# Placing weight rounding, head scalings and gate loads in the mixer stage of a one-layer hybrid decoder trunk

## The chip, the cores and the metric

The kernel runs on one core of one Trainium2 chip. The metric is the device time of one execution in microseconds, as the median of several runs. A core has five engines with instruction queues of their own: TensorE (PE, matmuls; its weight loads are listed as PEld), VectorE (DVE), ScalarE (ACT), GpSimd (POOL) and SyncE (SP, which here issues most DMAs). They meet only at semaphores. Matmul results land in PSUM, which has eight banks here.

## The reference, cut to what matters

One decoder layer over 1024 tokens and 16 meta tokens, width 1024, in float32. The change touches the mixer, whose parts are four recurrent heads, four pooling groups, and two gated branch products that are added and projected:

```python
u = rmsnorm(h, mix_norm_pre[l])
proj = u @ w_in[l]
q, f_logit, i_in, g_out, v_pool, gate_a, gate_b = jnp.split(proj, cuts, axis=-1)
a = hgrn2(q, f_logit, i_in, g_out, lbs[l], hgrn_out_norm[l])   # 4 heads of 128, chunks of 64; rmsnorm per head, times sigmoid(g)
p = multiscale_pool(v_pool, pool_proj[l], pool_scale[l])       # 4 groups of 128
z = (jax.nn.sigmoid(gate_a.astype(jnp.float32)) * (a @ w_branch_hgrn[l])
     + jax.nn.sigmoid(gate_b.astype(jnp.float32)) * (p @ w_branch_pool[l]))
h = h + rmsnorm(z @ w_out[l], mix_norm_post[l])
u = rmsnorm(h, ffn_norm_pre[l])
gt = causal_dwconv(u @ ffn_w_gate[l], ffn_conv_w[l], ffn_conv_b[l])
y = (jax.nn.gelu(gt, approximate=True) * (u @ ffn_w_up[l])) @ ffn_w_down[l]
h = h + rmsnorm(y, ffn_norm_post[l])
```

## The kernel before

**Precision.** Each matmul operand is split into a rounded high part and a low part (fp32r): `hi` is a cast on ACT, `lo = x - hi` a subtraction on DVE. A product is then three matmuls (hi by hi, lo by hi, hi by lo). In the profile these are `whi`/`wlo` for weights, `ah`/`al` for the heads' outputs, `uhi` for the pooled projections (high and low part lie in one buffer), `rh`/`rl` for a head's squares, `zc` for the merged branches. This splitting of weights is called rounding here. `whi`, `wlo` and the unrounded `wraw` each have three buffers in rotation.

**The stage.** Between 325 and 562 us of the profiled execution a string, `ORDER`, sets in which sequence the kernel's code is written, and for PE also the sequence in which it runs: there PE runs under a manual schedule, while ACT, DVE and SP get their order from a scheduler that follows the written order and its own estimates. The words of the string:

- `h0` to `h3`: one step of a head's generator (`head_steps`, L656 to L812). Its levels multiply `q`, `k` by decays `f` on DVE (L681, L687, L689), PE makes `sl`, and DVE copies it into `near` (L719); later PE transposes k (`pt`, copied by ACT to `kt`, L760), builds `ds`, DVE adds it up in the states `st` (L779), and PE makes the output `po` (L796, L797), which ACT copies to `o` (L799). At the end ACT and DVE square and split, PE sums the squares (`ms`, L806), ACT takes Ln and Exp into `rs` (L808, L809), and DVE scales (`o *= rs`, L810).
- `PV`, `G`, `PP`: value and gate products and the pool projections. `PP`'s results have posts on ACT (L847) and DVE (L848).
- `BB`, `BA`: the 8 branch products of the pool side and the 8 of the head side, in column blocks of 128; a and b are their halves. Their weights come in pairs, one load for two products, rounded by `wsplit2` (L166 ACT, L167 DVE), three loads ahead. After each product DVE multiplies the gates by it (`post_branch`, L886). The gates (`sa`) are loaded from DRAM (`sscr`) by `load_gate`. BA's posts are followed by the sum of both branches (L1249, L1268).
- `sa0` to `sa3`: the split of a finished head's output into `ah` and `al` (L840, L841).
- `w0` to `w5`: steps that round weights of the later FFN and put them into DRAM (`kept0h` to `kept9l`), with ACT casts (L929), DVE subtractions and combinations (L927, L930) and stores on SP (L944).

After the last branch product, BA7, comes the mix: products `pm` of the merged branches with w_out, from 561 us.

Of the kernel before, what the change touches and what calls it, by code (L numbers as in the profile page):

```python
# [12 lines left out]
ALU = mybir.AluOpType  # L13
# [41 lines left out]

ORDER = ("h0 h1 PVp0 PVq0 h0 PVr0 h1 PVs0 h0 PVp1 h1 PVq1 h0 PVr1 h1 PVs1 h0 sp0 PVp2 h1 PVq2 h0 sp1 PVr2 h1 PVs2 "
# [4 lines left out]
POOLED = ()  # L61
VLOAD = 8
TRUNC = False
# [2 lines left out]
CH_Q = [(0, CW), (CW, CW), (2 * CW, CW)]  # L66


@with_exitstack
def trunk_kernel(ctx: ExitStack, tc: tile.TileContext, x, meta_tokens, mix_norm_pre,  # L70
                 mix_norm_post, w_in, hgrn_lower_bounds, hgrn_out_norm, w_branch_hgrn,
                 pool_proj, pool_scale, w_branch_pool, w_out, ffn_norm_pre, ffn_norm_post,
                 ffn_w_gate, ffn_w_up, ffn_conv_w, ffn_conv_b, ffn_w_down, out):
    nc = tc.nc
    act, dve, pool_e, pe = nc.scalar, nc.vector, nc.gpsimd, nc.tensor

    cnt = [0]
    const = ctx.enter_context(tc.tile_pool(name="const", bufs=1))
# [27 lines left out]
    def bank(name="ps"):  # L106
        return stage["ps", "p"].tile([P, 512], F32, tag="ps", name=nm(name))
# [14 lines left out]
    def rr(a):  # L122
        return a.bitcast(F32)
# [23 lines left out]
        return t  # L147


    def wsplit(src, n_k, n_c, eng=dve):  # L150
        raw = wst.tile([P, n_k * n_c], F32, tag="wraw", name=nm("wraw"), bufs=NRAW, padded_shape=[P, 1024])
        with tc.issue_after(stage["after"].ins) if "after" in stage else nullcontext():
            stage["load"] = nc.sync.dma_start(raw.rearrange("p (k c) -> p k c", k=n_k), src)
        hi = wst.tile([P, n_k * n_c], F32R, tag="whi", name=nm("whi"), padded_shape=[P, 1024])
        lo = wst.tile([P, n_k * n_c], F32R, tag="wlo", name=nm("wlo"), padded_shape=[P, 1024])
        act.copy(hi, raw)
        eng.tensor_tensor(lo, raw, rr(hi), ALU.subtract)
        return [(hi.rearrange("p (k c) -> p k c", k=n_k), lo.rearrange("p (k c) -> p k c", k=n_k))]

    def wsplit2(*srcs):  # L160

        raw, (hi, lo) = wraw_tile(), (wst.tile([P, 1024], F32R, tag=t, name=nm(t)) for t in ("whi", "wlo"))
        views = [[t[:, i * 512 : (i + 1) * 512].rearrange("p (k c) -> p k c", k=4) for t in (raw, hi, lo)] for i in range(2)]
        for (r, _, _), src in zip(views, srcs):
            stage["load"] = nc.sync.dma_start(r, src)
        act.copy(hi, raw)  # L166
        dve.tensor_tensor(lo, raw, rr(hi), ALU.subtract)  # L167
        return [(h, l) for _, h, l in views]

    class Loader:  # L170


        def __init__(self, srcs, get=wsplit, first=None):
            self.srcs, self.get, self.got, self.at = srcs, get, [], 0
            self.ahead(first)
# [5 lines left out]
        def next(self):  # L181
            self.at += 1
            return self.got[self.at - 1]
# [475 lines left out]
    def head_steps(h):  # L659
        f, k, kb, q = slot(NM + L, name="f"), slot(NM + L, name="k"), slot(NM + L, name="kb"), slot(NM + L, name="q")  # L660
# [122 lines left out]
        o, rs = slot(TQ, name="o"), slot(TQ, name="rs")  # L783
# [7 lines left out]
        for j in range(2):  # L791
            ps = bank("po")
            for i in range(4):
                c = 4 * j + i
                t = M0 + c * P
# [11 lines left out]
            pe.matmul(ps[:, :n], onesr, rl[:, lo : lo + n], start=False, stop=True)  # L807
            act.activation(rs[:, lo : lo + n], ps[:, :n], AF.Ln, bias=eps_t)  # L808
        act.activation(rs, rs, AF.Exp, scale=-0.5)  # L809
        dve.tensor_tensor(o, o, rs, ALU.mult)  # L810
        heads[h] = dict(o=o)


# [24 lines left out]
    def split(src, name, eng=dve):  # L838
        hi, lo_ = slot(TQ, F32R, name + "h"), slot(TQ, F32R, name + "l")
        act.copy(hi, src)  # L840
        eng.tensor_tensor(lo_, src, rr(hi), ALU.subtract)  # L841
        return hi, lo_
# [10 lines left out]
    sas, sbs, z = {}, {}, {}  # L853
# [64 lines left out]
    def keep(*what, lo=None):  # L918

        tiles_ = [wst.tile([P, 1024], F32R, tag="whi", name=nm("whi"))]  # L920
        tiles_.append(wst.tile([P, 1024], F32R, tag="wlo", name=nm("wlo")) if lo is None else lo)
        at = [KEPT.index(key) for key, _ in what]
        for i, (_, src) in enumerate(what):
            hi, lo = (t[:, i * 512 : (i + 1) * 512].rearrange("p (k c) -> p k c", k=4) for t in tiles_)
            if isinstance(src, tuple):
                for a, op, b in src:
                    dve.tensor_tensor(rr(lo), rr(lo) if a is None else a, rr(lo) if b is None else b, op)  # L927
                src = rr(lo)
            act.copy(hi, src)  # L929
            dve.tensor_tensor(lo, src, rr(hi), ALU.subtract)  # L930
        for h, t in enumerate(tiles_):
            if len(at) == 2 and at[1] == at[0] + 1 and at[0] % 2 == 0:
                owed.append((kept[at[0] // 2][h], rr(t)))
                continue
            for i, n in enumerate(at):
                c = (n % 2) * 512
                owed.append((kept[n // 2][h][:, c : c + 512], rr(t)[:, i * 512 : (i + 1) * 512]))
# [34 lines left out]
    order = ORDER.split()  # L972
    order = [(o_[:-1], int(o_[-1])) for o_ in order]
# [59 lines left out]
    with tc.manual_schedule(engines={E.Activation, E.DVE, E.PE}):  # L1033
# [131 lines left out]
        for h in range(EARLY_G):  # L1165
            src, n_k, xs, chunks, post = job("G", h)
# [37 lines left out]
    def split_z(c, k):  # L1204
        n = len(TILES[c]) * P
        a = HALO + TILES[c][0] * P
        zc = slot(2 * n + (2 * HALO if c == 0 else 0), F32R, "zc")
        zh, zl = zc[:, :n], zc[:, n : 2 * n]
        act.copy(zh, z[k][:, a : a + n])
        dve.tensor_tensor(zl, z[k][:, a : a + n], rr(zh), ALU.subtract)  # L1210
        if c == 0:
            zm = zc[:, 2 * n :]
            act.copy(zm[:, :HALO], z[k][:, :HALO])
            dve.tensor_tensor(zm[:, HALO:], z[k][:, :HALO], rr(zm[:, :HALO]), ALU.subtract)
            return zh, zl, zm
        return zh, zl
# [3 lines left out]
    with tc.manual_schedule(engines={E.PE}):  # L1220
        for kind, i in order:
            if kind == "sp":
                pool_split(i)
                continue
            if kind == "w":
                keep_first(i) if i < EARLY else next(keeps[i - EARLY])
                continue
            if kind == "sa":
                ahl[i] = split(heads[i]["o"], "a")
                continue  # L1230
            if kind == "h":
                if i not in gens:
                    gens[i] = head_steps(i)
                next(gens[i], None)
                if not loader.at and "after" in stage:
                    loader.ahead()
                continue
            kind, part = kind.rstrip("abpqrs"), kind[-1]
            src, n_k, xs, chunks, post = job(kind, i)
            if part in "qr":  # L1240
                next(halves_of[kind, i])
                continue
            if part in "bs":
                banks = next(halves_of[kind, i])
                loader.ahead()
                pay()
                after[kind, i] = post(banks)
                if kind == "BA":
                    dve.tensor_tensor(sas[i], sas[i], sbs[i], ALU.add)  # L1249
                    z[i] = sas[i]  # L1250
                continue
            if kind in ("BA", "BB"):
                load_gate(sas if kind == "BA" else sbs, kind == "BB", i)
            ws = loader.next()
            if (kind, i) == ("BA", KD - 1):
                z0 = [split_z(0, k) for k in range(ZA)]
            if part in "ap":
                halves_of[kind, i] = proj_parts(None, 0, n_k, xs, chunks, ws=ws, name="p" + kind.lower(),
                                                cuts=(n_k // 2,) if part == "a" else range(n_k // 4, n_k, n_k // 4))
                next(halves_of[kind, i])  # L1260
                continue
            banks = proj(None, 0, n_k, xs, chunks, ws=ws, name="p" + kind.lower(),
                         by_bank=2 if (kind, i) == ("BA", KD - 1) else 0)
            loader.ahead()
            pay()
            after[kind, i] = post(banks)
            if kind == "BA":
                dve.tensor_tensor(sas[i], sas[i], sbs[i], ALU.add)  # L1268
                z[i] = sas[i]


    if TRUNC:
        close_pool("ps", "sm", "fm")
# [618 lines left out]
```

## The time and the profile before

| | |
|---|---|
| median of 3 runs | 1309.5 us (1308.31 to 1310.21) |
| profiled execution | 1310.05 us, span 1308.3 us |
| mean granted clock of TensorE | 0.996 |
| busy: PE / DVE / ACT / POOL | 1291.9 / 965.3 / 527.2 / 356.1 us |
| HBM | 174 MB read, 95 MB written, 206 GB/s over the span |

The stages in the trace: norm and values 0 to 66 us, gates 66 to 90, gates by Strassen's scheme 90 to 325, the stage of `ORDER` 325 to 562, mix 562 to 662, FFN by Strassen's scheme 662 to 1092, the projection down 1092 to 1308.

In a row of the timeline stand the start in us, the length, the engine, the line, the operation, output and inputs by the program's names, the size, how many, and in brackets the idle time before it and what ended that. A row of the waits has the engine with its line, what it waited for, the sum in us, the count and the longest. In a row of the windows stand the stretch, its length, each engine's busy time with its instructions, the granted clock, the DMA share and GB/s.

### The profile page before, as it was taken

The page shows a single profiled execution, that of the slowest core. Times are in us where ns is not written, and L with a number is a line of the kernel's source. Part 1 is how long each engine was busy: PE and PEld are TensorE (multiplying, and loading weights), DVE is VectorE, ACT ScalarE, POOL GpSimd, SP SyncE. Part 2 cuts the span into 40 slices and gives each one's busy share as a digit, 9 for nine tenths or more (in the row PEclk, how much of TensorE's full clock was granted, in tenths as well). Part 3 has the DMA queues.
Part 4 walks back from the last instruction along what each step waited for, and adds up shares of the span by engine and source line. Part 5 has one row for each costly group of instructions (what it writes and reads, how often), then busy time and mean ns, then how long its engine had stood idle before and what let it go on. Part 6 is the DMA issues. An engine that isn't in the chain of part 4 may idle for free.

```text
span 1308.3 us, 21993 instructions
## 1 busy us (share of the span) xinstructions
PE 1291.9 (99%) x8651; PEld 1140.8 (87%) x8651; DVE 965.3 (74%) x1311; ACT 527.2 (40%) x918; POOL 356.1 (27%) x308
## 2 busy tenths in 40 slices
PE   8999999999999999999999999999999999999998
PEld 7799899999999899978898888888888888888887
DVE  6768965454776877765588999888898985455758
ACT  6554433332244546235563222322322232444443
POOL 3015333130000000150045655553755552000000
PEclk9999999999999999999999999999999999999999
DMA  8135542325524767776777787568777799666644
GB/s 277 42 106 164 194 158 102 122 89 153 170 67 144 231 236 238 281 224 242 242 257 249 192 222 176 172 181 207 167 180 169 154 247 294 209 225 226 227 173 161
DMA packets 143817, 247.62 MB, mean 189 GB/s; under 512 B 11008, under 2 KB 75180, under 8 KB 143714
## 3 DMA queue, kind: packets, MB, share of 16 engines
q1 hardware_dynamic: 127026, 213.42, 48.7%
q0 software_dynamic: 12064, 24.38, 11.3%
q10 hardware_dynamic: 4624, 8.41, 1.7%
q8 instruction: 68, 1.11, 0.4%
q14 instruction: 35, 0.29, 0.1%
HBM read 174.12 MB, written 95.09 MB: 206 GB/s over the span
## 4 chain that ended last, share of the span: by engine, by line
PE 95%; DVE 1%; ACT 1%; DMA 1%; issue 0%; POOL 0%; DVEq 0%; ACTq 0%; SPq 0%; POOLq 0%
PE P L310 17%; PE P L311 17%; PE P L313 17%; PE pd L190 5%; PE pd L191 5%; PE pd L192 5%; PE pm L190 2%; PE pm L192 2%; PE pm L191 2%; PE ppv L210 1%; PE ppv L214 1%; PE ppv L211 1%; PE pba L210 1%; PE pba L211 1%; PE pg L210 1%; PE pv L192 1%
## 5 line engine op out<-in xcount | busy, mean ns | idle before, releaser
L311 PE MATMUL P<-v,whi 128*128 128x512 f32 (+2 forms) x408 | 140.7, 353 | 0.0
L310 PE MATMUL P<-v,whi 128*128 128x512 f32 (+2 forms) x408 | 140.7, 352 | 0.0
L313 PE MATMUL P<-v,wlo 128*128 128x512 f32 (+2 forms) x424 | 135.1, 349 | 0.0
L281 POOL TENSOR_TENSOR swa<-wraw,wraw 128x512 f32<-128x512 f32 x32 | 48.9, 1530 | 188.0 <-DMA wraw<-in_w_in_dram 77.3
L255 ACT CAST whi<-wraw 128x512 fp32r<-128x512 f32 x90 | 53.1, 618 | 101.5 <-PE P L311 86.9
L1602 DVE TENSOR_TENSOR rot<-wraw,rot 128x1024 fp32r<-128x1024 f32 x31 | 38.0, 1225 | 72.2 <-ACT rot L1601 72.2
L310 PEld LDWEIGHTS P<-v,whi 128*128 128x128 f32 x408 | 76.7, 188 | 10.4
L311 PEld LDWEIGHTS P<-v,whi 128*128 128x128 f32 x408 | 76.6, 188 | 10.2
L313 PEld LDWEIGHTS P<-v,wlo 128*128 128x128 f32 x424 | 74.0, 188 | 10.8
L192 PE MATMUL pd<-rot 128*128 128x512 f32 x274 | 82.5, 388 | 0.0
L191 PE MATMUL pd<-rot 128*128 128x512 f32 x274 | 82.5, 388 | 0.0
L190 PE MATMUL pd<-rot 128*128 128x512 f32 x274 | 81.9, 388 | 0.1
L256 DVE TENSOR_TENSOR wlo<-wraw,whi 128x512 fp32r<-128x512 f32 x86 | 74.5, 889 | 2.7 <-ACT whi L255 2.7
L255 ACT CAST whi<-swa 128x512 fp32r<-128x512 f32 x64 | 38.2, 619 | 91.9 <-PE P L311 81.2
L256 DVE TENSOR_TENSOR wlo<-swb,whi 128x512 fp32r<-128x512 f32 x64 | 67.9, 1068 | 9.0 <-ACT whi L255 8.7
L1601 ACT CAST rot<-wraw 128x1024 fp32r<-128x1024 f32 x31 | 32.7, 1054 | 90.8 <-PE pd L192 89.4
L310 PE MATMUL P<-uhi,whi 128*128 128x258 f32 (+2 forms) x240 | 68.6, 303 | 0.0
L311 PE MATMUL P<-ulo,whi 128*128 128x258 f32 (+2 forms) x240 | 68.4, 303 | 0.0
L255 ACT CAST whi<-swb 128x512 fp32r<-128x512 f32 x64 | 38.1, 618 | 69.3 <-PE P L311 61.0
L310 PE MATMUL P<-t2h,whi 128*128 128x258 f32 (+2 forms) x228 | 65.3, 304 | 0.3 <-DVE sg L869 0.3
L310 PE MATMUL P<-t4h,whi 128*128 128x258 f32 (+2 forms) x228 | 65.5, 304 | 0.0
L311 PE MATMUL P<-t4l,whi 128*128 128x258 f32 (+2 forms) x228 | 65.4, 304 | 0.0
(399 smaller groups left out, 3849.3 us busy)
## 6 DMA issues: line engine op xcount, KB each, us to landing
wraw<-in_w_in_dram SPq DMA_DIRECT2D x36, 512.0 KB, 4.5
yt<-ysum SPq DMA_DIRECT2D x33, 512.0 KB, 5.3
wraw<-in_ffn_w_gate_dram SPq DMA_DIRECT2D x26, 512.0 KB, 7.1
wraw<-in_ffn_w_up_dram SPq DMA_DIRECT2D x22, 512.0 KB, 6.8
wsum<-in_ffn_w_down_dram SPq DMA_DIRECT2D x22, 512.0 KB, 8.2
wraw<-in_w_out_dram SPq DMA_DIRECT2D x18, 512.0 KB, 5.1
ysum<-ys SPq DMA_DIRECT2D x11, 768.0 KB, 6.4
sa<-sscr SPq DMA_DIRECT2D x16, 513.0 KB, 7.1
```

What stands on the lines that cost most here:

```text
L190: pe.matmul(ps, ahi, bhi, start=first, stop=False)
L191: pe.matmul(ps, ahi, blo, start=False, stop=False)
L192: pe.matmul(ps, alo, bhi, start=False, stop=last)
L210: pe.matmul(ps[:, :n], whi[:, k, :], xhi, start=(k == 0), stop=False)
L255: act.copy(hi, src)
L256: (pool_e if 4 <= i < 2 * self.early else dve).tensor_tensor(lo, src, rr(hi), ALU.subtract)
L281: pool_e.tensor_tensor(s1, a21, a22, ALU.add)
L310: pe.matmul(d, whi[:, k, :], xh[:, c : c + w], start=(k == 0 and onto is None), stop=False, **go)
L311: pe.matmul(d, whi[:, k, :], xl[:, c : c + w], start=False, stop=False, **go)
L313: pe.matmul(x[:, o : o + w], wlo[:, k, :], xh[:, c : c + w], start=False, stop=(k == 3), **go)
L1601: act.copy(hi, src)
L1602: dve.tensor_tensor(lo, src, rr(hi), ALU.subtract)
```

## The change

1. ACT and DVE are wrapped so that each remembers its last instruction. After the posts of products, after head steps and after the splits of heads, `mark()` notes these as urgent. Within `behind()` an instruction is ordered behind the last urgent one on ACT and on DVE; this is an order within an engine's queue and adds no semaphore. It is put around the rounding in `wsplit`, `wsplit2` and `keep`, and around the heads' last scaling, which becomes a step of its own with a `yield` ahead of it.
2. `load_gate` is called one branch product ahead.
3. `ORDER` gets the extra `h` steps for those yields; `sa2` stands ahead of BBa7 instead of BBb7, `sa3` ahead of BAa0, and the last `w5` behind BAb1.
4. Ahead of BA7 a PSUM tile, "spare", is taken from the pool and one column of it is set to zero on DVE.

```diff
-         "Gr3 h2 PP1 Gs3 h3 PP2 h2 PP3 h3 BBa0 h1 h2 BBb0 h3 w0 BBa1 h2 BBb1 h3 w1 BBa2 h2 BBb2 h3 w2 BBa3 h2 h3 w3 "
-         "BBb3 h2 h3 w4 BBa4 w4 BBb4 h2 h3 w4 BBa5 sa0 w5 BBb5 h3 sa1 w5 BBa6 h2 w5 BBb6 BBa7 h3 sa2 BBb7 BAa0 BAa1 "
-         "sa3 w5 BAb0 BAb1 BA2 BA3 BA4 BA5 BA6 BA7")
+         "Gr3 h2 PP1 h0 Gs3 h3 PP2 h2 PP3 h3 BBa0 h1 h2 BBb0 h1 h3 w0 BBa1 h2 BBb1 h3 w1 BBa2 h2 BBb2 h3 w2 BBa3 h2 "
+         "h3 w3 BBb3 h2 h3 w4 BBa4 w4 BBb4 h2 h3 w4 BBa5 sa0 w5 BBb5 h3 sa1 w5 BBa6 h2 w5 BBb6 h2 sa2 BBa7 h3 BBb7 "
+         "h3 sa3 BAa0 BAa1 BAb0 BAb1 w5 BA2 BA3 BA4 BA5 BA6 BA7")
...
-    act, dve, pool_e, pe = nc.scalar, nc.vector, nc.gpsimd, nc.tensor
+    act, dve, pool_e, pe = Traced(nc.scalar), Traced(nc.vector), nc.gpsimd, nc.tensor
...
+    urgent = {}
+
+    def mark():
+        urgent.update((e, e.last) for e in (act, dve))
+
+    def behind():
+        order = ExitStack()
+        for ins in urgent.values():
+            order.enter_context(tc.issue_after(ins.ins))
+        return order
...
     def wsplit2(*srcs):
...
-        act.copy(hi, raw)
-        dve.tensor_tensor(lo, raw, rr(hi), ALU.subtract)
+        with behind():
+            act.copy(hi, raw)
+            dve.tensor_tensor(lo, raw, rr(hi), ALU.subtract)
...
         act.activation(rs, rs, AF.Exp, scale=-0.5)
-        dve.tensor_tensor(o, o, rs, ALU.mult)
+        yield
+        with behind():
+            dve.tensor_tensor(o, o, rs, ALU.mult)
...
             if kind == "sa":
                 ahl[i] = split(heads[i]["o"], "a")
+                mark()
                 continue
...
-                next(gens[i], None)
+                if next(gens[i], True) is None:
+                    mark()
...
                 after[kind, i] = post(banks)
+                mark()
...
             if kind in ("BA", "BB"):
-                load_gate(sas if kind == "BA" else sbs, kind == "BB", i)
+                at = branch.index((kind, i))
+                for b_, m in branch[at : at + 2] if at == 0 else branch[at + 1 : at + 2]:
+                    load_gate(sas if b_ == "BA" else sbs, b_ == "BB", m)
             ws = loader.next()
             if (kind, i) == ("BA", KD - 1):
+                dve.memset(bank("spare")[:, :1], 0.0)
                 z0 = [split_z(0, k) for k in range(ZA)]
...
+    urgent.clear()
```

`Traced` passes every call on to the engine and keeps what it returned (`dma_start` excepted). In the changed program all instructions of ACT and DVE therefore bear the line of that wrapper, L81, and are told apart by their tiles.

PE's order is the same in both programs, and so is POOL's; the order on DVE, ACT and SP differs within the stage of `ORDER` only. Three places on DVE follow. In the rows `L848` or `uhi<-ppp` is PP's post, `wlo<-wraw,whi` of width 1024 a rounding of branch weights, of width 512 one of FFN weights.

DVE around PP2's posts (ppp_604 to ppp_606), ahead of BBa0, before:

```order
L719 COPY_PREDICATED near_589_4701<-mask2_148,sl_603_4859 128x64x2
L167 TENSOR_TENSOR wlo_615_4969<-wraw_613_4967,whi_614_4968 128x1024
L689 TENSOR_TENSOR f_563_4551<-f_563_4551 128x264
L681 TENSOR_TENSOR k_538_4376<-k_538_4376,f_537_4375 128x66x8
L848 SCALAR_TENSOR_TENSOR uhi_6_90<-ppp_604_4896,par_126,uhi_6_90 128x342
L687 TENSOR_TENSOR q_540_4378<-q_540_4378,f_537_4375 128x64x8
L719 COPY_PREDICATED near_556_4481<-mask8_162,sl_609_4918 128x16x8
L848 SCALAR_TENSOR_TENSOR uhi_6_90<-ppp_605_4897,par_126,uhi_6_90 128x342
L848 SCALAR_TENSOR_TENSOR uhi_6_90<-ppp_606_4898,par_126,uhi_6_90 128x342
```

The same place after:

```order
L81 COPY_PREDICATED near_589_4701<-mask2_148,sl_603_4859 128x64x2
L81 SCALAR_TENSOR_TENSOR uhi_6_90<-ppp_604_4896,par_126,uhi_6_90 128x342
L81 TENSOR_TENSOR f_563_4551<-f_563_4551 128x264
L81 SCALAR_TENSOR_TENSOR uhi_6_90<-ppp_605_4897,par_126,uhi_6_90 128x342
L81 TENSOR_TENSOR k_538_4376<-k_538_4376,f_537_4375 128x66x8
L81 TENSOR_TENSOR q_540_4378<-q_540_4378,f_537_4375 128x64x8
L81 SCALAR_TENSOR_TENSOR uhi_6_90<-ppp_606_4898,par_126,uhi_6_90 128x342
L81 COPY_PREDICATED near_556_4481<-mask8_162,sl_609_4918 128x16x8
L81 TENSOR_TENSOR wlo_615_4969<-wraw_613_4967,whi_614_4968 128x1024
```

The rounding wlo_615 moved from ahead of the first post to behind the third.

DVE in the state steps of the second pair of heads (`st`), before:

```order
L779 SCALAR_TENSOR_TENSOR st_692_5622<-st_692_5622,f_563_4551,ds_694_5626 128x128
L930 TENSOR_TENSOR wlo_707_5678<-wraw_704_5673,whi_706_5677 128x512
L930 TENSOR_TENSOR wlo_707_5678<-wraw_705_5675,whi_706_5677 128x512
L779 SCALAR_TENSOR_TENSOR st_692_5622<-st_692_5622,f_563_4551,ds_695_5635 128x128 x2
L167 TENSOR_TENSOR wlo_710_5703<-wraw_708_5701,whi_709_5702 128x1024
L779 SCALAR_TENSOR_TENSOR st_692_5622<-st_692_5622,f_563_4551,ds_695_5635 128x128
```

The same place after:

```order
L81 SCALAR_TENSOR_TENSOR st_693_5624<-st_693_5624,f_563_4551,ds_695_5628 128x128
L81 TENSOR_TENSOR wlo_685_5559<-wraw_677_5524,wlo_685_5559 128x512
L81 SCALAR_TENSOR_TENSOR st_693_5624<-st_693_5624,f_563_4551,ds_695_5628 128x128
L81 SCALAR_TENSOR_TENSOR st_693_5624<-st_693_5624,f_563_4551,ds_696_5637 128x128 x2
L81 TENSOR_TENSOR wlo_685_5559<-wlo_685_5559,whi_684_5558 128x512
L81 SCALAR_TENSOR_TENSOR st_693_5624<-st_693_5624,f_563_4551,ds_696_5637 128x128
```

The 1024 wide rounding left the gap ahead of the last state step, and a 512 wide one of an FFN unit, in two steps, stands between the states.

DVE around head 3's split (al from o_711, after: o_712) ahead of BAb0's posts (`sa<-sa,pba`), before:

```order
L810 TENSOR_TENSOR o_711_5717<-o_711_5717,rs_712_5718 128x1026
L886 TENSOR_TENSOR sa_731_5837<-sa_731_5837,pbb_734_5841 128x342
L927 TENSOR_TENSOR wlo_730_5799<-wraw_705_5675,wlo_730_5799 128x512
L930 TENSOR_TENSOR wlo_730_5799<-wlo_730_5799,whi_729_5798 128x512
L841 TENSOR_TENSOR al_752_5953<-o_711_5717,ah_751_5952 128x1026
L930 TENSOR_TENSOR wlo_730_5799<-wlo_730_5799,whi_729_5798 128x512
L167 TENSOR_TENSOR wlo_742_5898<-wraw_740_5896,whi_741_5897 128x1024
L886 TENSOR_TENSOR sa_743_5906<-sa_743_5906,pba_744_5908 128x342
```

The same place after, up to the first of BAb0's posts:

```order
L81 TENSOR_TENSOR o_712_5719<-o_712_5719,rs_713_5720 128x1026
L81 TENSOR_TENSOR al_733_5840<-o_686_5593,ah_732_5839 128x1026
L81 TENSOR_TENSOR wlo_722_5755<-wlo_722_5755,whi_721_5754 128x512
L81 TENSOR_TENSOR wlo_731_5800<-wraw_705_5675,wraw_706_5677 128x512
L81 TENSOR_TENSOR wlo_731_5800<-wraw_705_5675 128x512
L81 TENSOR_TENSOR wlo_722_5755<-wlo_722_5755,whi_721_5754 128x512
L81 TENSOR_TENSOR al_745_5909<-o_712_5719,ah_744_5908 128x1026
L81 TENSOR_TENSOR wlo_731_5800<-wlo_731_5800,wraw_705_5675 128x512
L81 TENSOR_TENSOR wlo_731_5800<-wlo_731_5800,whi_730_5799 128x512
L81 TENSOR_TENSOR wlo_731_5800<-wraw_706_5677,wlo_731_5800 128x512
L81 TENSOR_TENSOR sa_734_5843<-sa_734_5843,pba_747_5914 128x342
```

Head 2's split and four half roundings stand between head 3's scaling and its split; the 1024 wide rounding (wlo_742, now wlo_743) is no longer ahead of the posts, and follows them and the addition of the two branches.

More of the change, by code (lines that the diff above doesn't have):

```diff
@@ L66, with __init__, __getattr__, issue @@
 CH_Q = [(0, CW), (CW, CW), (2 * CW, CW)]
+class Traced:
+    def __init__(self, engine):
+        self.engine, self.last = engine, None
+    def __getattr__(self, name):
+        method = getattr(self.engine, name)
+        if not callable(method) or name == "dma_start":
+            return method
+        def issue(*a, **k):
+            self.last = method(*a, **k)
+            return self.last
+        return issue
 @with_exitstack
@@ L155, in wsplit @@
         lo = wst.tile([P, n_k * n_c], F32R, tag="wlo", name=nm("wlo"), padded_shape=[P, 1024])
-        act.copy(hi, raw)
-        eng.tensor_tensor(lo, raw, rr(hi), ALU.subtract)
+        with behind():
+            act.copy(hi, raw)
+            eng.tensor_tensor(lo, raw, rr(hi), ALU.subtract)
         return [(hi.rearrange("p (k c) -> p k c", k=n_k), lo.rearrange("p (k c) -> p k c", k=n_k))]
@@ L165, in wsplit2 @@
             stage["load"] = nc.sync.dma_start(r, src)
-        act.copy(hi, raw)
-        dve.tensor_tensor(lo, raw, rr(hi), ALU.subtract)
+        with behind():
+            act.copy(hi, raw)
+            dve.tensor_tensor(lo, raw, rr(hi), ALU.subtract)
         return [(h, l) for _, h, l in views]
@@ L809, in head_steps @@
         act.activation(rs, rs, AF.Exp, scale=-0.5)
-        dve.tensor_tensor(o, o, rs, ALU.mult)
+        yield
+        with behind():
+            dve.tensor_tensor(o, o, rs, ALU.mult)
         heads[h] = dict(o=o)
@@ L922, in keep @@
         at = [KEPT.index(key) for key, _ in what]
[L923 to L930, printed above, removed]
+        with behind():
+            for i, (_, src) in enumerate(what):
+                hi, lo = (t[:, i * 512 : (i + 1) * 512].rearrange("p (k c) -> p k c", k=4) for t in tiles_)
+                if isinstance(src, tuple):
+                    for a, op, b in src:
+                        dve.tensor_tensor(rr(lo), rr(lo) if a is None else a, rr(lo) if b is None else b, op)
+                    src = rr(lo)
+                act.copy(hi, src)
+                dve.tensor_tensor(lo, src, rr(hi), ALU.subtract)
         for h, t in enumerate(tiles_):
@@ L1266, in trunk_kernel @@
             after[kind, i] = post(banks)
+            mark()
             if kind == "BA":
```

## The prediction

> **What bounds the kernel now.** I read the page's busy times first, then the chain that ended last, then TensorE's waits, then the granted clock window by window.
>
> ```profile
> PE 1291.9 (99%) x8651; PEld 1140.8 (87%) x8651; DVE 965.3 (74%) x1311; ACT 527.2 (40%) x918; POOL 356.1 (27%) x308
> PE 95%; DVE 1%; ACT 1%; DMA 1%; issue 0%; POOL 0%; DVEq 0%; ACTq 0%; SPq 0%; POOLq 0%
> ```
>
> TensorE (PE) is busy 99% of the span and makes 95% of the chain. Its instructions and their order stay the same, so the change can only shorten or make gaps in PE, and through them move the clock. The gaps of the stage that it touches (325 to 562 us; us in total, times, longest):
>
> ```profile
> PE po L797 <- DVE st L779: 2.0, 1, 2.0
> PE pbb L210 <- DVE uhi L848: 1.7, 1, 1.7
> PE sl L698 <- DVE q L687: 0.9, 1, 0.9
> PE ms L806 <- ACT rs L808: 0.6, 1, 0.6
> PE pbb L210 <- DVE near L719: 0.3, 1, 0.3
> ```
>
> They make 5.6 us, in the rows' hundredths further down. Windows of 3.4 us (start:end, length, busy PE, PEld, DVE, ACT, POOL, then granted clock, DMA share, GB/s) show what two of them cost besides:
>
> ```profile
> 434.80:438.20 3.40, 1.35 (x18) 0.88 (x7) 3.40 (x8) 3.38 (x7) 0.00 (x0) 1.00 1.06 331
> 438.20:441.60 3.40, 3.40 (x14) 3.40 (x14) 3.40 (x8) 0.47 (x1) 0.00 (x0) 0.50 1.08 370
> ...
> 465.50:468.90 3.40, 2.46 (x23) 2.15 (x22) 3.09 (x7) 0.47 (x2) 0.00 (x0) 1.00 1.06 399
> 496.20:499.60 3.40, 1.36 (x12) 1.08 (x10) 1.90 (x4) 1.22 (x2) 0.00 (x0) 1.00 0.85 326
> 499.70:503.10 3.40, 3.40 (x13) 3.40 (x14) 2.99 (x4) 2.79 (x4) 0.00 (x0) 0.50 0.52 154
> ```
>
> A window with 3.40 - 1.35 = 2.05 us of PE idle (434.8), and one with 2.04 (496.2), is each followed by 3.4 us at a clock of 0.50: half of 3.4, 1.7 us of work, is lost each time. The window with 0.94 idle (465.5) is followed by full clock.
>
> The Trainium skill ("TensorE: Matmul & The Clock Gate", Part 1: The HAM clock gate) states free-running windows of 3413 ns, with which the 3.4 here agrees, and a clock that halves after an idle window, with the advice to keep gaps below about 3.4 us. Here 2.04 us of idle sufficed, so the rows decide. By the page's rule no gap of this stage would cost clock, and the gain summed below would be 3.4 us smaller.
>
> The sum stands against the profiled execution's own time, 1310.05 us (span 1308.3), which is 0.55 above the median of the runs, 1309.5, and within their 1308.31 to 1310.21.
>
> **Place A: rounding and the pool projections' posts.** BBa0, the first branch product, needs PSUM banks that PP2's three posts (L847 on ACT, then L848 on DVE) free.
>
> ```profile
> 432.64 1.06 ACT L166 CAST whi<-wraw 128x1024 fp32r<-128x1024 f32 x1
> 433.57 1.44 ACT L847 ACTIVATE uhi<-ppp,par 128x342 fp32r<-128x342 f32 x3
> ...
> 433.73 1.23 DVE L167 TENSOR_TENSOR wlo<-wraw,whi 128x1024 fp32r<-128x1024 f32 x1 [0.58 <-ACT whi L166]
> 434.87 0.63 DVE L689 TENSOR_TENSOR f<-f 128x264 f32<-128x264 f32 x1
> 435.42 0.70 DVE L681 TENSOR_TENSOR k<-k,f 128x528 f32<-128x528 f32 x1
> 436.04 0.56 DVE L848 SCALAR_TENSOR_TENSOR uhi<-ppp,par,uhi 128x342 fp32r<-128x342 f32 x1
> 436.52 0.68 DVE L687 TENSOR_TENSOR q<-q,f 128x512 f32<-128x512 f32 x1
> ...
> 436.65 0.42 PE L210 MATMUL pbb<-uhi,whi 128*128 128x342 f32 x1 [1.74 <-DVE uhi L848]
> 437.55 0.39 PE L210 MATMUL pbb<-uhi,whi 128*128 128x342 f32 x1 [0.31 <-DVE near L719]
> ```
>
> The rounding (1.06 on ACT, then 0.58 of waiting and 1.23 on DVE) stood ahead of all three posts and now stands behind them; f is between the first and the second, k and q between the second and the third. Laid end to end (DVE starts the next some 0.08 before the last one's end): ACT's first post 432.7 to 433.25, DVE's to 433.8, f to 434.35, the second post to 434.85, k and q to 436.0, the third to 436.5. PE could start at 436.65 - 1.74 = 434.91 and needs the second bank 0.31 later and the third 0.62 later, at 435.53: 1.0 us idle where 2.05 was. Bounds: 0.3 (k and q early) and 2.05 (nothing won). 1.0 is nearer to 0.94 than to 2.04, so the clock stays. The rounding moved is for BB2 and BB3, two products later, which covers it. The norm's wait of ms for ACT, 0.64 in this place, is of the same chain of DVE and ACT and stays near 0.5.
>
> **Place C: sl waits for q, 0.94.** On DVE a half rounding and three posts of sa come ahead of it:
>
> ```profile
> 465.67 0.69 DVE L930 TENSOR_TENSOR wraw<-wraw,whi 128x512 fp32r<-128x512 f32 x1
> ...
> ACT whi L929 <- DMA kept1h<-whi: 4.5, 1, 4.5
> ACT whi L929 <- DMA kept3h<-whi: 0.4, 1, 0.4
> ```
>
> The posts still do; the half rounding goes. I leave 0.4, the shorter of ACT's waits for a store of rounded weights, since these roundings now run some us later and a buffer can be short; bounds 0 and 1.5.
>
> **Place D: head 2's states.** The last state product waited for a rounding (of BA0's and BA1's weights) that itself waited 1.33 for ACT, which waited for a DMA.
>
> ```profile
> 495.79 0.59 ACT L799 COPY o<-po 128x512 f32<-128x512 f32 x1 [1.56 <-PE po L797]
> 496.91 1.04 ACT L166 CAST whi<-wraw 128x1024 fp32r<-128x1024 f32 x1 [0.53 <-DMA wraw<-in_w_branch_hgrn_dram]
> ...
> 497.98 1.23 DVE L167 TENSOR_TENSOR wlo<-wraw,whi 128x1024 fp32r<-128x1024 f32 x1 [1.33 <-ACT whi L166]
> ...
> 499.52 0.69 PE L797 MATMUL po<-q,st 128*128 128x128 f32 x2 [2.04 <-DVE st L779]
> ```
>
> It moves behind this head's states and BB6's posts. In its stead an FFN unit's roundings stand between the states. Ahead of the last one: ACT copies o until 496.4, casts half a tile (0.6 of the 1.06 above) until 497.0, DVE rounds its half (0.69) until 497.7, the state comes at 498.0; PE wants it at 499.52 - 2.04 = 497.5: 0.5. Ahead of the earlier ones there is again a DVE that waits for ACT, 1.3 as in the row of 497.98. Together 1.8, bounds 0.5 and 3.5. These gaps have products between them and spread over several us, so I take no half clock, though 1.8 in one window would be nearer to 2.04: the first rival.
>
> **The end of the stage: new waits.**
>
> ```profile
> 520.38 1.22 DVE L841 TENSOR_TENSOR al<-o,ah 128x1026 fp32r<-128x1026 f32 x1
> ...
> 522.12 1.22 DVE L167 TENSOR_TENSOR wlo<-wraw,whi 128x1024 fp32r<-128x1024 f32 x1
> 523.58 1.35 DVE L886 TENSOR_TENSOR sa<-sa,pba 128x342 f32<-128x342 f32 x3 [0.24 <-PE pba L214]
> ...
> 522.41 0.32 PE L211 MATMUL pba<-al,whi 128*128 128x342 f32 x1
> ...
> 560.91 0.39 PE L190 MATMUL pm<-whi,zc 128*128 128x512 f32 x1
> 561.11 0.51 DVE L886 TENSOR_TENSOR sa<-sa,pba 128x342 f32<-128x342 f32 x1 [0.45 <-PE pba L192]
> ```
>
> Head 3's al ends 0.8 us before PE reads it at 522.41. Head 2's al (1.1) and four half roundings (2.4) now come between its scaling and it, in place of a post and two halves (1.6): 1.9 later, so PE waits 1.1 (bounds 0 and 2.5). The wlo of BA2 and BA3 at 522.12 now follows BAb0's posts (1.35), a half rounding and an addition of 1.2: with the 1.1 of delay it ends at 523.58 + 1.1 + 1.3 + 0.6 + 1.1 + 1.2 = 528.9, and BA2's first low product is due 8 + 18 + 6 products of 0.16 after 522.41, with the same 1.1, at 528.6: 0.3, with the signal 0.4 (bounds 0 and 1.3). The mix's first product at 560.91 shared a PSUM bank with BA7's second part; the spare tile shifts the banks by one, it shares with the third, whose post ends at 561.62: 0.75 with the signal (bounds 0 and 0.8). The memset itself is one column, before BA7's posts, where DVE waits 0.45: nothing.
>
> **The other parts.** No row of PE's or DVE's waits names the gates' load (`sa<-sscr`), so one product ahead wins nothing. It stands earlier in SP's queue, ahead of weight loads and stores while DMA is full (share 1.06 to 1.08 above): 0, covered by weights loaded products ahead, bounds -0.3 and 1. The scalings of heads 0 and 1 have tens of us until BAa0: 0. The splits of heads' outputs come earlier only in the text; their place on DVE is what al's term counts. The danger is ACT's queue: w1 to w3's casts need whi buffers that are free when their stores land, and head 2's kt copies, for which PE waits, stand behind them.
>
> ```profile
> kept0h<-whi SPq DMA_DIRECT2D x2, 256.0 KB, 8.2
> kept1h<-whi SPq DMA_DIRECT2D x2, 256.0 KB, 4.5
> ```
>
> With landings of 4.5 the layout leaves these copies 1.3 us: 0. Upper bound: two casts at 8.2, 2 x (8.2 - 4.5 - 1.3) = 4.8.
>
> **The sum.** Lost now: A 2.05 + 0.64 + 1.7, C 0.94, D 2.04 + 1.7: 9.1. Left or new: A 1.0, ms 0.5, C 0.4, D 1.8, al 1.1, wlo 0.4, mix 0.75: 5.95. Gain 3.1: 1306.9 for the profiled execution, 1306.4 for the median. I forecast the median.
>
> **The rivals.**
> Half clock stays (no change): D's gaps, or A's with ms, meet in one window. One costs 1.7 (gain 1.4: 1308.1), two take it all (1309.8). For it: 1.8 nearer to 2.04. Against: A's 1.0 lies by 0.94, and D's gaps are several.
>
> ACT stalls behind kept stores (slower): the 4.8 above, with a half clock after each of the two gaps, 3.4: 8.2 more, 1314.6. It decides where it eats the gain and 2.6 more, 5.7: with stores landing in about 7 us (2 x (7 - 4.5 - 1.3) + 3.4 = 5.8). For it: 8.2 in the fullest stretch, and earlier gate loads beside it. Against: 4.5 right beside it, and the DMA share of 0.52 by 500.
>
> Nearly all goes: al, wlo and D's new rows find slack that the layout lacks, 3.3 of 5.95 less: 1303.1.
>
> It doesn't do what it says: a rounding is put behind what was marked when it was written, not behind later steps. If A keeps its 2.05 and half clock, 2.75 of the gain goes: 1309.2.
>
> **Numbers.** A measurement of this kernel can tell about 0.2%, 2.6 us, from no change: faster is below 1306.9. Chances: forecast 0.52 (own range 1304.4 to 1307.6, of it 0.45 below 1306.9), half clock 0.18, slower 0.08, nearly all 0.12, not as it says 0.10. Faster 0.45 + 0.12 = 0.57; same 0.07 + 0.18 + 0.10 = 0.35; slower 0.08. The range 1302.4 to 1310.0 leaves out the slower case, a little of two half clocks and the best end.
>
> **What the changed profile would show.** Right: clock 1.00 over 434 to 442 and 496 to 503; PE's wait for PP2's posts about 1.0; at most 0.4 for q near 467; small waits for st, below 2 together; new waits of PE for al near 520 and for the post of BA7 at the mix's first product. Wrong: a clock of 0.50 in either place, PE waiting for kt or ds behind ACT's casts, or a wait for al above 2.5.

## The result and the profile after

The changed kernel is faster: 1305.23 us median of 11 runs (1304.06 to 1307.15) against 1308.77 for 11 runs of the kernel before, a ratio of 0.9976 with a 95% interval of 0.9969 to 0.9984. By the ratio that is 3.1 us (2.1 to 4.1); the medians lie 3.5 apart. The forecast was 1306.4. Two executions of e5 below (2129 us, at a granted clock of 0.56) and two of the kernel before that ran beside the experiments (1586 and 7292 us) are far longer than the rest, and the ratios leave them out.

The page after has the same work on PE, 4 us shorter:

```profile
PE 1287.9 (99%) x8651; PEld 1136.6 (87%) x8651; DVE 963.0 (74%) x1312; ACT 526.8 (40%) x918; POOL 354.1 (27%) x308
```

PE's waits after 335 us within the stage (us, times, longest). The five gaps of before, 5.6 us, are now five others, 3.7 us:

```profile
PE pba L242 <- DVE al L81: 1.1, 1, 1.1
PE pbb L241 <- DVE uhi L81: 0.8, 1, 0.8
PE pm L221 <- DVE sa L81: 0.7, 1, 0.7
PE pba L245 <- DVE wlo L81: 0.6, 1, 0.6
PE po L828 <- DVE st L81: 0.5, 2, 0.3
```

The windows of the changed kernel at the same two places (BBa0, then head 2's states). The clock is 1.00 in all of them:

```profile
431.50:435.00 3.50, 2.72 (x76) 2.15 (x75) 3.50 (x8) 3.48 (x7) 0.00 (x0) 1.00 0.99 345
435.00:438.40 3.40, 3.32 (x24) 3.04 (x23) 3.40 (x7) 1.60 (x3) 0.00 (x0) 1.00 1.11 351
488.00:491.40 3.40, 2.94 (x24) 2.56 (x23) 3.24 (x10) 1.29 (x3) 0.00 (x0) 1.00 0.52 154
491.40:494.80 3.40, 3.20 (x23) 3.01 (x23) 1.70 (x4) 2.32 (x4) 0.00 (x0) 1.00 0.83 316
```

The two profiled executions lie 6.0 us apart (1310.05 and 1304.06), almost twice what the medians say. The timelines of PE show where. The first value product, and a score product early in the stage, of the kernel before (the mix's first product, at 560.91, stands in the prediction); then the same two of the changed kernel, the four products that wait longest from there on, and the last of them is the mix's first:

```profile
9.48 0.50 PE L190 MATMUL pv<-whi,uhi 128*128 128x512 f32 x1 [0.46 <-ACT uhi L1072]
335.96 0.75 PE L727 MATMUL sb<-q,kb 128*32 128x32 f32 x64 [0.49 <-issue]
```

```profile
8.01 0.50 PE L221 MATMUL pv<-whi,uhi 128*128 128x512 f32 x1 [0.46 <-ACT uhi L81]
334.10 0.75 PE L758 MATMUL sb<-q,kb 128*32 128x32 f32 x64 [0.49 <-issue]
...
434.72 0.42 PE L241 MATMUL pbb<-uhi,whi 128*128 128x342 f32 x1 [0.78 <-DVE uhi L81]
514.54 0.42 PE L242 MATMUL pba<-al,whi 128*128 128x342 f32 x1 [1.13 <-DVE al L81]
520.49 0.76 PE L245 MATMUL pba<-ah,wlo 128*128 128x342 f32 x3 [0.60 <-DVE wlo L81]
554.86 0.47 PE L221 MATMUL pm<-whi,zc 128*128 128x512 f32 x1 [0.70 <-DVE sa L81]
```

1.5 us of the 6.0 are there before 10 us, and 1.86 at 335 us, in stages that the change does not touch: that is the start, and it differs from execution to execution (334.06 to 336.15 in the eleven profiles of the experiments). From there to the mix's first product the kernel before takes 560.91 - 335.96 = 224.95 us and the changed one 554.86 - 334.10 = 220.76: 4.2 less. This length of the stage is used below beside the medians.

### The profile page after: what moved, and what is told of

It is laid out like the page before. It is cut to its first block, busy times and chain, and to the rows that moved or that the text cites. A ratio compares the mean times of both kernels' runs of the same rounds, so it can differ in the third digit from the quotient of the medians.

```text
span 1302.4 us, 21989 instructions
## 1 busy us (share of the span) xinstructions
PE 1287.9 (99%) x8651; PEld 1136.6 (87%) x8651; DVE 963.0 (74%) x1312; ACT 526.8 (40%) x918; POOL 354.1 (27%) x308
## 4 chain that ended last, share of the span: by engine, by line
PE 93%; DVE 2%; ACT 2%; DMA 1%; issue 0%; SPq 0%; POOL 0%; DVEq 0%; ACTq 0%; POOLq 0%
PE P L341 17%; PE P L342 17%; PE P L344 17%; PE pd L221 5%; PE pd L223 5%; PE pd L222 5%; PE pm L221 2%; PE pm L223 2%; PE pm L222 2%; PE ppv L241 1%; PE ppv L245 1%; PE ppv L242 1%; PE pg L241 1%; PE pv L223 1%; PE pg L242 1%; PE pv L221 1%
## 5 line engine op out<-in xcount | busy, mean ns | idle before, releaser
L81 ACT CAST whi<-wraw 128x512 fp32r<-128x512 f32 (+2 forms) x140 | 97.0, 714 | 163.6 <-PE P L342 87.7
L81 DVE TENSOR_TENSOR p<-p,P 128x512 f32<-128x512 f32 (+2 forms) x122 | 83.3, 683 | 44.1 <-PE P L344 43.2
L81 DVE TENSOR_TENSOR wlo<-wraw,whi 128x512 fp32r<-128x512 f32 (+2 forms) x110 | 95.9, 891 | 11.3 <-ACT whi L81 7.0
L81 DVE TENSOR_TENSOR rot<-wraw,rot 128x1024 fp32r<-128x1024 f32 x31 | 37.9, 1224 | 72.3 <-ACT rot L81 72.2
L81 ACT CAST whi<-swa 128x512 fp32r<-128x512 f32 x64 | 38.1, 619 | 92.3 <-PE P L342 81.8
L81 DVE TENSOR_TENSOR wlo<-swb,whi 128x512 fp32r<-128x512 f32 x64 | 65.9, 1037 | 9.5 <-ACT whi L81 9.5
L81 ACT CAST rot<-wraw 128x1024 fp32r<-128x1024 f32 x31 | 32.7, 1054 | 90.8 <-PE pd L223 89.4
L81 ACT CAST whi<-swb 128x512 fp32r<-128x512 f32 x64 | 38.1, 618 | 69.3 <-PE P L342 63.3
```

Source lines behind the costliest of these rows:

```text
L81: self.last = method(*a, **k)
```

## The experiments

All times are medians; the ratio is to the kernel before on the same chip. The kernel before had medians of 1308.3 to 1308.5 us beside the experiments and 1308.8 beside the changed kernel, so medians of different rounds compare to about half a microsecond. The length of the stage is worked out as above, from one profiled execution. An edge is an order that `behind()` sets.

| run | us | ratio (95%) | stage, us |
|---|---|---|---|
| e1: changed, without edges around rounding | 1306.58 | 0.9985 (0.9976 to 0.9993) | 222.3 |
| e2: before, with these edges alone | 1308.02 | 1.0001 (0.9993 to 1.0010) | 224.6 |
| e3: changed, without the spare tile | 1305.74 | 0.9981 (0.9972 to 0.9990) | 221.3 |
| e4: changed, w5 later, spare tile ahead of BA5 | 1302.62 | 0.9954 (0.9941 to 0.9968) | 217.9 |
| e5: changed, 1.2 us more on DVE at BBa0 | 1308.25 | 0.9999 (0.9990 to 1.0008) | 222.3 |
| e6: changed, 2.4 us more on DVE at BBa0 | 1305.84 | 0.9984 (0.9975 to 0.9993) | 221.8 |
| e7: changed, splits in their old places | 1305.74 | 0.9981 (0.9972 to 0.9990) | 220.5 |
| e8: changed, gates at their own product | 1309.15 | 1.0008 (0.9999 to 1.0017) | 223.6 |
| e9: before, with early gates alone | 1308.67 | 1.0001 (0.9992 to 1.0010) | 224.4 |
| e10: before, with the edges and early gates | 1307.84 | 0.9991 (0.9982 to 1.0000) | 222.8 |
| e11: changed, without edges around scalings | 1308.18 | 0.9999 (0.9990 to 1.0008) | 224.0 |

### e1 and e2: the edges around rounding, taken away and alone

```diff
 e1, in wsplit, wsplit2 and keep of the changed kernel:
-        with behind():
+        with nullcontext():
 e2: the kernel before, with Traced, mark(), behind() and only these three "with behind()"
```

> The changed kernel without the order edges around the rounding of weights (branch weights and kept weights); the head scalings' edges, gates one ahead, written order and spare tile stay. Theory (the edges around rounding make the gain, by keeping a gap of about 2 us out of a clock window): the rounding stands ahead of PP2's posts again, PE's wait at BBa0 is back at 1.5 to 2.1 us, one or two stretches of 3.4 us at a clock of 0.50, and the median is within 1.5 us of the kernel before. Rival (the extra head steps and the new written order make the gain): wait at BBa0 stays below 1.0, no half clock there, median within 1 us of the changed kernel.

> The kernel before plus only the order edges around the rounding of weights: written order, gates, head scalings and banks as before, no spare tile. Theory: wait at BBa0 0.7 to 1.0, clock 1.00 throughout the stage, median 3 to 4 us below the kernel before. Rival (written order): median within 1 us of the kernel before.

Waits of PE, e1 and then e2:

```profile
PE pbb L241 <- DVE uhi L81: 1.6, 1, 1.6
PE po L828 <- DVE st L81: 1.5, 1, 1.5
...
```

```profile
PE po L828 <- DVE st L81: 2.5, 2, 1.4
PE ms L837 <- ACT rs L81: 2.2, 1, 2.2
PE pbb L241 <- DVE uhi L81: 0.9, 1, 0.9
PE pm L221 <- DVE sa L81: 0.7, 1, 0.7
```

Without the edges the gap at BBa0 is back (1.6 and 0.3 instead of 0.78), with one half clock behind it. Between the medians 1.35 us of the gain are lost (1306.58 and 1305.23); that size is uncertain, since the intervals of the two ratios overlap (0.9976 to 0.9993 and 0.9969 to 0.9984). The edges alone do at BBa0 what they should (0.87) and gain nothing: the states wait 2.5 us, and head 3's squares 2.2, with a half clock after the latter. So the edges are needed, and not enough. Of each theory half came true: e1's gap and half clock and e2's wait at BBa0 are as expected, but e1 does not lose the whole gain, and e2 gains nothing.

### e3: the spare tile

```diff
-                dve.memset(bank("spare")[:, :1], 0.0)
```

> The changed kernel without the spare tile ahead of BA7. The prediction said that the spare tile causes the wait of 0.7 us at the mix's first product. By that: wait gone, 0.7 us faster. Rival (the rotation of banks comes out of the changed order of the stage, and the third part of BA7 is in the mix's banks with the spare tile or without): the wait of 0.7 stays, same time within 0.5 us.

The wait of 0.7 us at the mix's first product stays without the spare tile, so the tile as placed is worth nothing that can be measured (1305.74 against 1305.23). The wait goes with the edges around rounding: every kernel with them has it, e2 too, which has no spare tile (e4 is the exception, below), and the three without them, the kernel before, e9 and e1, do not, though e1 has the tile. The built programs point to the reason. The first result of the mix lies in banks 0 and 1 in all of them; the third part of BA7 lies in bank 1 wherever PE waits, and in bank 3 where it does not. The tile only swaps the banks of the first and the second part.

### e7, e8, e9: the splits' places and the gates

```diff
 e7: "... BBb6 BBa7 h3 h2 sa2 BBb7 BAa0 BAa1 h3 sa3 w5 BAb0 BAb1 BA2 ..."
 e8: load_gate(sas if kind == "BA" else sbs, kind == "BB", i)   as before
 e9: the kernel before, with the changed load_gate loop alone
```

> The changed kernel with sa2, sa3 and the last w5 back in their old places in the written order (the extra head steps stand directly ahead of the splits). Theory (the splits' new places are worth nothing by themselves; what holds head 3's split up is the w5 work queued ahead of it, which is there in both): al waited for 1 us or more, time within 0.7 us of the changed kernel. Rival (the early split pays): 1 us or more slower.

> The changed kernel with the branch gates loaded at their own product, as before. Theory: nothing waits for the gates in either kernel, so the time stays within 0.7 us of the changed kernel, apart from what the scheduler shifts on DVE. Rival (the earlier loads free SP's queue at the time when weights and stores need it): waits for weights or kept stores return, 1.5 us or more slower.

> The kernel before with only the gates loaded one product ahead. Theory A (early loads matter only together with the edges around rounding: they let the posts of the last pool products be planned early, so that head 3's squares get three banks; in the kernel before they had three banks anyway, and its gaps at BBa0 and in the states have other causes): the gaps of 1.7 and 2.0 us stay, median within 1 us of the kernel before. Theory B (the early loads are the main gain by themselves): 3 us faster or more.

The splits' places are worth nothing measurable. The gates are worth the whole gain: without their early loads the kernel is 3.9 us slower than the changed one, yet alone (e9) they gain nothing, with the two long gaps and their half clocks as in the kernel before. Waits of e8, on PE and then on DVE:

```profile
PE ms L837 <- ACT rs L81: 2.4, 1, 2.4
PE pba L241 <- DVE sa L81: 1.3, 1, 1.3
...
DVE sa L81 <- DMA sa<-sscr: 0.2, 1, 0.2
```

No more than 0.2 us in the stage is a wait for a gate to land. What changed is the order on DVE and the use of PSUM. With late gates BB7's posts (sa, 514.03 in the next rows) stand behind head 2's split and half roundings, where the changed kernel has them ahead of that split; PE waits 1.3 us for them. And the third sum of head 3's squares waits until ACT has read the first:

```profile
505.82 0.98 ACT L81 ACTIVATE rs<-ms,eps_t 128x342 f32<-128x342 f32 x2
...
506.42 0.42 PE L837 MATMUL ms<-rh,onesr 128*128 128x342 f32 x1 [2.44 <-ACT rs L81]
...
511.62 1.23 DVE L81 TENSOR_TENSOR al<-o,ah 128x1026 fp32r<-128x1026 f32 x1 [0.47 <-ACT ah L81]
512.76 0.69 DVE L81 TENSOR_TENSOR wlo<-wlo,wraw 128x512 f32<-128x512 f32 x1
513.36 0.68 DVE L81 TENSOR_TENSOR wlo<-wlo,whi 128x512 fp32r<-128x512 f32 x1
514.03 1.35 DVE L81 TENSOR_TENSOR sa<-sa,pbb 128x342 f32<-128x342 f32 x3
```

ACT's first read ends at about 505.82 + 0.55, and PE goes on at 506.42. In the built programs of e8 and e2 the first and the third of head 3's sums have the same PSUM bank (4, 0, 4), in those of the changed kernel and of e10 three (4, 0, 2). e2 and e10 differ in the early gates alone, and so do e8 and the changed kernel; in both pairs the wait (2.2 and 2.4 us) is there with the shared bank and gone without it. That the scheduler puts posts later because it estimates a later gate, and picks the bank for that reason, is an inference from the programs; no run set the banks alone.

### e10 and e11: the edges with early gates, and the scalings

```diff
 e10: e2 with the changed load_gate loop
 e11, at the end of head_steps of the changed kernel:
         yield
-        with behind():
+        with nullcontext():
             dve.tensor_tensor(o, o, rs, ALU.mult)
```

> The kernel before with the edges around rounding and the gates one product ahead; written order, head scalings and banks as before. Theory A (these two together make the gain): wait at BBa0 0.7 to 0.9, no wait at head 3's squares, no half clock in most executions, median 2.5 to 3.5 us below the kernel before. Theory C (the head steps and the new places of the splits are needed as well): waits of 1.5 us or more are left in the states or at the squares, gain below 1.5 us.

> The changed kernel without the edges around the heads' last scaling (the extra head steps stay). Theory A: nothing waits for the order of the scalings, same time within 0.7 us. Theory C: 1 us or more slower.

With both, head 3's squares no longer wait, and the gain is 1.2 us by the ratio (0.0 to 2.4), 0.6 between the medians. Theory C holds: the states wait 1.8 us in e10 and 2.4 in e11, where the changed kernel has 0.5. The clock window of e11 in which the longest of these waits lies, and the next one:

```profile
490.00:493.40 3.40, 1.65 (x10) 1.27 (x11) 3.36 (x9) 1.70 (x3) 0.00 (x0) 1.00 0.75 278
493.40:496.80 3.40, 3.40 (x17) 3.40 (x17) 1.83 (x5) 1.59 (x4) 0.00 (x0) 0.50 0.94 343
```

The second window has the half clock. Product by product it puts e11 back by 1.3 us; with the states' 1.9 us more of waiting (2.4 less 0.5) that is 3.2, against 3.3 us between e11's stage and the changed kernel's, and 3.0 between the medians. DVE's rows say why the states are late, e11 first, then the changed kernel:

```profile
484.85 0.69 DVE L81 TENSOR_TENSOR wlo<-wraw,wraw 128x512 f32<-128x512 f32 x1 [2.11 <-DMA kept5l<-wlo]
...
486.06 1.22 DVE L81 TENSOR_TENSOR rl<-rs,rh 128x1026 fp32r<-128x1026 f32 x1
487.20 0.34 DVE L81 SCALAR_TENSOR_TENSOR st<-st,f,ds 128x128 f32<-128x128 f32 x1
```

```profile
482.71 1.22 DVE L81 TENSOR_TENSOR rl<-rs,rh 128x1026 fp32r<-128x1026 f32 x1
483.85 0.34 DVE L81 SCALAR_TENSOR_TENSOR st<-st,f,ds 128x128 f32<-128x128 f32 x1
484.12 0.69 DVE L81 TENSOR_TENSOR wlo<-wraw,wraw 128x512 f32<-128x512 f32 x1
...
```

In e11 an FFN unit's first subtraction stands ahead of the first state and holds DVE for 2.11 us, until the store kept5l has freed its buffer; in the changed kernel it stands behind it and the store is done. e10 has the same order with a wait of 1.43. What the scaling's edge does is thus to move this rounding by a few places in the planned order. That it is this wait, and not another difference of the two orders, was not tested by a run of its own.

### e5 and e6: a longer gap at BBa0

```diff
+ ahead of PP2's third post, and ordered ahead of it:
+ dve.tensor_tensor(uhi_f[:, 7 * LP : 7 * LP + 1026], rr(a[:, :1026]), rr(a[:, :1026]), ALU.mult)    (e6: 2100 columns)
```

> The changed kernel with one extra DVE product of 1026 columns (about 1.2 us) ahead of PP2's third post; its result is overwritten by PP3's posts. PE's gap at BBa0 grows from 0.78 to about 2.0 us. Theory (the granted clock looks at fixed windows of 3.413 us, and 3.4 us at half clock follow only a window with more than 1.5 to 1.6 us of idle): with the grid where the changed kernel's profile has it, a boundary at 434.96, the gap is split into about 1.0 and 1.0 and no half clock follows: 1.2 us more than the changed kernel in the profile; where the gap lies in one window, 2.9 more. Rival (a single gap of 2 us always halves the clock): 0.50 for 3.4 us, 2.9 more. Rival by the notes' rule (only gaps above 3.4 us): never.

> As e5_gap_one, with an extra DVE product of 2100 columns (about 2.4 us): PE's gap at BBa0 about 3.1 us. Theory: wherever the grid lies, one window then holds at least 1.55 us of the idle time, in most positions more than 1.6: 3.4 us at 0.50 follow in nearly every execution, 2.4 + 1.7 = 4.1 us more than the changed kernel. Rival (only gaps above 3.4 us halve the clock): 2.4 more.

e6 did not make the gap it was to make: with the longer operation DVE's order was planned anew, PE's wait split into 0.8 ahead of the head's `sl` products and 0.9 at BBa0, and nothing follows from it for the clock; its theory stays untested. In e5 the gap is 1.99 us, and the profiled execution shows the clock windows (boundaries 433.3, 436.7, 440.1) cutting it in two:

```profile
433.30:436.70 3.40, 1.97 (x72) 1.44 (x70) 3.40 (x7) 3.38 (x6) 0.00 (x0) 1.00 0.98 328
436.70:440.10 3.40, 2.79 (x16) 2.51 (x16) 3.40 (x9) 0.47 (x2) 0.00 (x0) 1.00 1.09 340
```

1.4 us of idle in the one and 0.6 in the other, and no half clock. The median is 3.0 us above the changed kernel's, though the gap grew by 1.2 us only and the profiled stage by 1.5. A half clock in most of the other executions would come near it, but the granted clocks on record speak against that: one half clock takes 0.0013 of an execution's mean clock, the low clock at the very end takes another 0.0005 to 0.0016 in every trace here, and six of e5's nine ordinary executions have 0.999 or 1.000 (the changed kernel has 0.998 or 0.999). Where the rest of the 3.0 us comes from stays open.

### e4: what was left

```diff
-... h3 sa1 w5 BBa6 h2 w5 BBb6 h2 sa2 BBa7 h3 BBb7 h3 sa3 BAa0 BAa1 BAb0 BAb1 w5 BA2 BA3 BA4 BA5 BA6 BA7
+... h3 sa1 BBa6 h2 BBb6 h2 sa2 BBa7 h3 BBb7 h3 sa3 BAa0 BAa1 BAb0 BAb1 BA2 w5 BA3 w5 BA4 w5 BA5 BA6 BA7
 the spare tile ahead of BA5 instead of BA7
```

> The changed kernel with three of the four w5 steps put behind BA2, BA3 and BA4, and the spare tile taken ahead of BA5 instead of BA7. Theory (what is left in the changed kernel is work queued ahead of head 3's split and of BA2's rounding, and one shared bank): PE's wait for al 0 to 0.4 instead of 1.13, for wlo 0 instead of 0.60, at the mix 0 instead of 0.70: 2.0 to 2.4 us faster than the changed kernel. Rival: the moved stores and roundings meet the head of the mix or the start of the FFN, new waits of 1 us or more appear after 530 us, and the time is that of the changed kernel or above.

```profile
PE ppp L245 <- issue: 0.7, 1, 0.7
PE po L828 <- DVE st L81: 0.7, 2, 0.5
...
```

The run makes two edits at once and does not tell their parts apart; in its program the third part of BA7 lies in bank 3. The three waits at the end of the stage are gone and no new one came after 530 us. The median is 1302.62 over 5 runs, the ratio 0.9954 (0.9941 to 0.9968): 6.0 us below the kernel before and 2.6 below the changed one. The wait at BBa0 (0.8) is not in this list either; a wait of 0.7 that has no releaser, in the product ahead of it, takes its place. This is the fastest version.

## Why the prediction was right, and where it was not

The forecast's frame held: PE's order did not change, the two long gaps and their half clocks were what could be won, and the end of the stage gave part of it back. Term by term, as predicted and as the profiled execution after has it: A 1.0 and 0.78; ms 0.5 and 0; C 0.4 and 0; D 1.8 and 0.31 + 0.20 = 0.51; al 1.1 and 1.13; wlo 0.4 and 0.60; mix 0.75 and 0.70. Left in all 5.95 and 3.7.

The total came out near the forecast partly by luck. By the profiles the stage is 4.2 us shorter, by the medians the kernel is 3.1 to 3.5 faster. The trace of before that the sum was made against had two half clocks, and not every execution of that kernel has: two of them leave a mean clock of 0.9974 at most, and 32 of the 85 ordinary executions beside the experiments show 0.998 or 0.999. (One of the 85 shows 0.947 and is no longer than the others, which stays unexplained.)

The sum's 9.1 lost and the 3.7 that is left would make 5.4 us, not 4.2. Each product's start in the kernel before, less its start in the changed one and less the 1.86 us at 335 us, shows where the rest went. The changed kernel is ahead by 3.3 us behind place A, 4.4 behind C and 7.3 behind D, and then loses 1.4 at al, 0.8 at wlo and 0.9 at the mix. So a half clock was priced too high: the two cost 1.5 us each, not 1.7 (rows in the last section). And a wait costs somewhat more than its row says, 1.4 where al's row has 1.13.

The term that was furthest off is D's. "Ahead of the earlier ones there is again a DVE that waits for ACT, 1.3" was taken from a row of another rounding; no such wait came, and what can come there is a wait for a store (1.43 in e10, 2.11 in e11), which the change's order avoids. A half clock at D, the first rival, did not come in the changed kernel, and came in e10 and e11, so the rival was a close one.

Two steps failed in their reasons. "One product ahead wins nothing" for the gates: it asked only whether something waits for their landing. e8 shows 3.9 us, through the places that the posts get on DVE and through a shared PSUM bank. "The scalings of heads 0 and 1 have tens of us until BAa0: 0": e11 shows 3 us, through the place of another instruction. In both, the working priced the moved instruction and not what the scheduler does with everything else. The third: the wait at the mix was put down to the spare tile, and e3 shows that it is there without it. That the size was right says nothing for the cause.

The rivals: stores did not stall kt's copies in the changed kernel. "It doesn't do what it says" was wrong for the rounding at BBa0. Against the Trainium skill's advice ("TensorE: Matmul & The Clock Gate", Part 1: The HAM clock gate) that only gaps above about 3.4 us matter, 1.56 us in one window was enough in e10 and 1.61 in e1 (rows in the last section); its free-running window agrees with e5.

## What to carry to other kernels

Where a scheduler sets the order, an early load or a moved instruction acts through the plan even when nothing waits for it; a part that is worth nothing alone (e2, e9) can be needed by the others (e8, e11), so take parts away from the whole as well as adding them one by one. Price a gap of PE together with the clock window that it lies in. Look at the new waits last: here one more move of work that nobody needs soon, with the spare tile's, brought another 2.6 us (e4).

## What the hardware showed that was not expected

The half clock does not follow a gap but a window. Idle time of PE in a window of 3.4 us and the clock of the next: 1.51 us full (e1, 494.6), 1.56 half (e10, 489.8), 1.61 half (e1, 433.2), 1.72 full (e8, 504.7), 1.75 half (e11). So in these runs it turns between 1.5 and 1.75 us of 3.4, and the idle time as the trace gives it does not decide it alone; the ends of products are modelled there, so how exact these idle times are stays open. In e1, the window at BBa0 and a later one, each with its next:

```profile
433.20:436.60 3.40, 1.79 (x70) 1.28 (x68) 3.33 (x5) 3.40 (x9) 0.00 (x0) 1.00 0.99 339
436.60:440.00 3.40, 3.13 (x12) 2.94 (x11) 3.40 (x8) 1.59 (x2) 0.00 (x0) 0.50 1.10 347
...
494.60:498.00 3.40, 1.89 (x16) 1.61 (x14) 2.18 (x5) 1.51 (x2) 0.00 (x0) 1.00 0.87 332
498.00:501.40 3.40, 3.40 (x24) 3.40 (x23) 3.15 (x5) 3.14 (x4) 0.00 (x0) 1.00 0.53 154
```

Then e10 and e8:

```profile
489.80:493.20 3.40, 1.84 (x14) 1.46 (x13) 3.29 (x10) 1.73 (x3) 0.00 (x0) 1.00 0.74 282
493.20:496.60 3.40, 3.40 (x16) 3.40 (x15) 1.90 (x4) 2.71 (x4) 0.00 (x0) 0.50 0.92 323
```

```profile
504.70:508.10 3.40, 1.68 (x11) 1.68 (x12) 3.40 (x7) 3.39 (x6) 0.00 (x0) 1.00 0.52 156
508.10:511.50 3.40, 3.40 (x23) 3.40 (x23) 2.88 (x5) 3.37 (x5) 0.00 (x0) 1.00 0.92 256
```

In e2 two adjacent windows had 1.2 and 1.4 us of idle, 2.6 together, and the clock stayed:

```profile
488.90:492.30 3.40, 2.20 (x16) 1.80 (x15) 3.40 (x6) 0.43 (x2) 0.00 (x0) 1.00 0.47 123
492.30:495.70 3.40, 1.98 (x15) 1.79 (x16) 3.29 (x10) 1.75 (x4) 0.00 (x0) 1.00 0.76 294
495.70:499.10 3.40, 3.40 (x26) 3.40 (x25) 1.90 (x4) 3.34 (x5) 0.00 (x0) 1.00 0.95 306
```

A window at half the clock costs less than half its length. The same three products of BBa0 and the start of the next one, in the kernel before at the half clock, then in the changed one at the full clock:

```profile
438.44 1.06 PE L214 MATMUL pbb<-uhi,wlo 128*128 128x342 f32 x3
439.30 0.49 PE L210 MATMUL pbb<-uhi,whi 128*128 128x342 f32 x1
```

```profile
435.14 0.63 PE L245 MATMUL pbb<-uhi,wlo 128*128 128x342 f32 x3
435.61 0.32 PE L241 MATMUL pbb<-uhi,whi 128*128 128x342 f32 x1
```

They take 0.86 us and 0.47, so of 3.41 us at the half clock 3.41 x (1 - 0.47 / 0.86) = 1.5 us are lost.

The start differs between executions of the same work: the first value product began at 8.01 to 9.48 us in the profiles of these kernels, and the stage at 334.06 to 336.15, which is as much as most of the parts tried here; a single pair of profiles would have shown twice the gain.
